# Scores in the groups' ring, late sum forms, a bias from a reversed table without transposes, and the mixers' fp32 products on fewer entries

## The chip, the cores and the metric

The kernel runs on one core of a Trainium2 chip. The metric is the device time of one execution in microseconds (us). The kernel before took 2042.75 us, the median of 3 runs (2042.73 to 2042.9). A profile is one more execution, taken by the hardware profiler, and it carries its own time.

## The reference

The block has one sequence of 256 frames with 2048 channels, all in fp32. A half-step SwiGLU FFN (2048 to 5632 and back) is followed by two token mixers side by side, a merge, a second half-step FFN and a last norm. The mixers are what the change touches:

```python
h = rmsnorm(x, norm_mix_g)
q_a, k_a, v_a, q_r, k_r, v_r, g_r, gate_a, gate_r = split(h @ w_in)
# attention: 8 heads of 128; chunks of 64 frames; a frame sees its whole chunk and the earlier chunks
scores = q_a k_a^T * 128 ** -0.5
rel_idx = clip(q_pos - k_pos, -128, 128) + 128
bias = rel_bias_table[:, rel_idx]              # table: 8 heads x 257
p = softmax(where(valid, scores + bias, -1e30))
att = p v_a
# retention: 8 heads of 128, rotary q and k, decay gamma_h ** |n - m|, the same chunk mask
ret = rmsnorm_per_head(sum over visible m of (q_r[n].k_r[m]) * decay * v_r[m])
merged = sigmoid(gate_a) * (att @ w_out_att) + sigmoid(gate_r) * ((silu(g_r) * ret) @ w_out_ret)
x = x + merged @ w_out
```

## The kernel before, in words

**Steps.** All large products run in fp32r: both factors are split in a high part (a rounded copy) and a low part (the rest), and three products (high by high, low by high, high by low: L148, L149, L151, in `three`) stand for one fp32 product. Weights come in slices of 256 rows by 512 columns (512 KB) on SyncE's queue (`fetch`); ScalarE makes the high part (L137), VectorE the low part (L138). One slice is one *step*: 12 matmuls of 512 columns on TensorE (a `Gemm` of 16 or 8 row blocks is 8 or 4 steps). A part of the GEMMs runs in *Strassen groups*, whose steps have 6 matmuls and need sums of weight slices and of activations instead. For these, copies of weight slices are loaded (L560, tiles named z...k and z...x) or added on the way (L565, L604) by GpSimd's DMA queue, and VectorE adds them (L549, L603, L617). There are 1080 steps.

**Order.** Every engine runs its instructions in the order in which the program writes them. The loop `run` goes over the steps: it first writes the splits for the step 4 ahead, then everything that is due at this step, in the order in which it was put on the list, and then the step's own products. `later(n, fn)` puts `fn` on the list for n steps later, and `at(step, fn)` for a given step. So all small work is placed by hand: its fp32 matmuls and transposes stand between the fp32r matmuls of two steps. Such a place is called an *entry* below.

**The mixers.** The steps that multiply with `w_in` begin at step 390. The last four projections, for retention (QR0, KR0, QR1, KR1, 8 steps each), begin at step 600, which is called M here. At M+32 begin the four output projections of attention (4 steps each), at M+48 those of retention, at M+64 the product with `w_out`, at M+96 the second FFN. In the stretch from M to M+48 the attention and the retention of all heads are inserted:
- Attention head h begins at M + HEAD_AT[h] (L48): `scores` (L966, L967: 256 and 128 columns of fp32 in a PSUM bank of the ring "side"; three VectorE operations scale the scores and add the bias), one step on `powers` (ScalarE), two on `shares` (VectorE), four on `transposes` (three, and a ScalarE copy at L1004), six on `values` (L1010, L1011).
- The results of a rotary projection are turned on VectorE and transposed by `to_transposed` (four transposes by L395 each) 3 and 4 steps after the projection's last step.
- Retention of four heads: b=0 is placed when KR0 is done and b=1 when KR1 is done, with a first wait RET_WAIT (L42). Head i has `scores` (L1035, L1036; VectorE multiplies by the decay at L1038 and L1039, giving the tile rp) at wait+2i, and `values` (L1048 to L1050, tile ro) three steps later. `finish`, at wait+9, for both halves of the frames: square (ScalarE), sum of squares (VectorE, L1060), a power on GpSimd (L386), and four VectorE products with the gate (L1066, tile rg). Three steps on, both halves of rg are transposed and split (`Operand.put`, tile retp).

**PSUM** has rings of banks: "acc" (3), "z" (3, used by the Strassen groups and by the second accumulator of ordinary jobs) and "side" (2, used by all the small work).

**The relative bias.** At 18 steps ahead of step 390, four DMAs of GpSimd's queue broadcast the 257 entries of two heads each to 128 partitions (`load_rel`); four steps later VectorE extends them to 384 entries (L344) and four DMAs (L349) write them to DRAM, as `rel_ext` [8, 128, 384]. Two DMAs at M-4 (L357, in `bias_transposed`) read that table with a row stride of 383, which gives the bias transposed (keys on partitions). From M on, `bias_natural` turns it: 16 transposes (L368, tile psb) at M to M+3, four at each step, four ScalarE copies (L374), four masking memsets (L375).

**Sums for Strassen.** A normalized activation operand (class `Norm`: n1, nm for the mixers, n2 for the second FFN) is written by `put` as transposed blocks b = 0 to 3. After each odd block, `add_up` makes four sum forms s5, s6, s3, s7 (L489 to L511), 1, 4, 7 and 10 steps later, each with one VectorE operation for the sum, a ScalarE copy for its high part 2 steps later, and a VectorE difference for its low part (L511) 3 steps later.

Of the kernel before, what the change touches and what calls it, by code (L numbers as in the profile page):

```python
# [8 lines left out]
F32 = mybir.dt.float32  # L9
F32R = mybir.dt.float32r  # L10
AF = mybir.ActivationFunctionType
ALU = mybir.AluOpType
# [3 lines left out]
P = 128  # L16
SEQ = 256
NT = SEQ // P
D = 2048
# [19 lines left out]
HALF_K = D // P // 2  # L39
LEAD = (10, 10)  # L40
MIX_LEAD = 6
RET_WAIT = (14, 5)  # L42
HELD = 6
MIX_ADDED = (0,)
FIRST_ADDED = (2, 3)
MIX_AHEAD = 12
FIRST_WAIT = 4
HEAD_AT = (3, 6, 10, 13, 17, 20, 24, 27)  # L48

MIX_SHARE = (0.5,) * 4 + (1.0,) * 4 + (0.0,) * 4 + (0.2,) * 4  # L50
# [33 lines left out]
def block_kernel(ctx: ExitStack, tc: tile.TileContext, x, g1, w1g, w1u, w1d, gm, w_in, rel, woa, wor, wo,  # L84
# [12 lines left out]
    def act_tile(dt, name):  # L97
        return apool.tile([P, 4, SEQ], dt, tag="act", name=name)
# [4 lines left out]
    def side_tile(name):  # L103
        return psum.tile([P, NB], F32, tag="side", name=name, bufs=2)
# [12 lines left out]
    def later(n, fn):  # L117
        due.setdefault(state["step"] + n, []).append(fn)
# [208 lines left out]
    nc.gpsimd.memset(mhalf, -0.5)  # L327

    rel_ext = dram.tile([HEADS, P, EXT], F32, name="rel_ext")
    REL_PAIR = 2  # L330

    def load_rel():

        tiles = []
        for h in range(0, HEADS, REL_PAIR):
            t = act_tile(F32, f"rel{h}").rearrange("p a q -> p (a q)")[:, : REL_PAIR * EXT]
            t = t.rearrange("p (h e) -> p h e", h=REL_PAIR)
            nc.gpsimd.dma_start(t[:, :, :NREL], rel[0, h : h + REL_PAIR, :].partition_broadcast(P))
            tiles.append(t)
        later(4, lambda: spread_rel(tiles))  # L340

    def spread_rel(tiles):
        for i, t in enumerate(tiles):
            nc.vector.tensor_copy(  # L344
                t[:, :, NREL:], t[:, :, NREL - 1 : NREL].to_broadcast([P, REL_PAIR, EXT - NREL])
            )

            dst = rel_ext[REL_PAIR * i : REL_PAIR * (i + 1)].rearrange("h p e -> p h e")
            nc.gpsimd.dma_start(dst, t)  # L349

    def bias_transposed():
        t = [act_tile(F32, f"biasT{half}") for half in range(2)]
        for half in range(2):
            src = bass.AP(
                rel_ext.tensor, rel_ext.offset + half * 4 * P * EXT + MAXREL, [[EXT - 1, P], [P * EXT, 4], [1, SEQ]]
            )
            nc.gpsimd.dma_start(t[half], src)  # L357
        return t

    def bias_natural(bt):  # L360
        for b in range(HEADS // 4):
            table["bias", b] = act_tile(F32, f"bias{b}")

        def turn(h):
            ps = side_tile(f"psb{h}")
            for i in range(2):
                for j in range(2):
                    nc.tensor.transpose(  # L368
                        ps[:, (2 * i + j) * P : (2 * i + j + 1) * P],
                        bt[(h + i) // 4][:, (h + i) % 4, j * P : (j + 1) * P],  # L370
                        id_sb,
                    )
            dst = table["bias", h // 4][:, h % 4 : h % 4 + 2, :]
            nc.scalar.copy(dst.rearrange("p h k -> p (h k)"), ps)  # L374
            nc.vector.memset(dst[0:CHUNK, :, CHUNK:P], MASKED)  # L375

        turn(0)
        for h in range(2, HEADS, 2):
            later(h // 2, lambda h=h: turn(h))


    def rsqrt(dst, ssum, n, width):

# [37 lines left out]
    class Norm:  # L421
# [40 lines left out]
        def put(self, b, halves=(0, 1)):  # L462
            if 0 in halves:
                self.raw[b] = act_tile(F32, f"{self.name}x{b}")
            raw = self.raw[b]
            for half in halves:
                ps = side_tile(f"{self.name}p{b}{half}")
                for i in range(2):
                    k = 4 * b + 2 * half + i
                    for t in range(NT):  # L470
                        nc.tensor.transpose(
                            ps[:, (2 * i + t) * P : (2 * i + t + 1) * P], xs[t][:, k * P : (k + 1) * P], id_sb
                        )
                for i in range(2):
                    k = 4 * b + 2 * half + i
                    nc.scalar.activation(
                        raw[:, 2 * half + i, :], ps[:, i * SEQ : (i + 1) * SEQ], AF.Copy, scale=self.gain[:, k : k + 1]
                    )
            k0, k1 = 2 * halves[0], 2 * halves[-1] + 2
            j = 4 * (b // 2)  # L480
            for t in range(NT):
                self.split_to(f"a{t}{b % 2}", slice(j + k0, j + k1), raw[:, k0:k1, t * P : (t + 1) * P])
            if 1 in halves and not self.sums:
                del self.raw[b]
            elif 1 in halves and b % 2 == 1:
                for i, key in enumerate(self.SUMS):
                    later(1 + 3 * i, lambda key=key: self.add_up(b // 2, key))

        def add_up(self, p, key):  # L489

# [420 lines left out]
    def ret_qk_done(key, b, after=None):  # L911
        def done(acc):
            srcs = []
            half = HD // 2

            def turn(t, s):
                r = tmp_tile(f"{key}{b}{t}r", "qk", 4)
                u = tmp_tile(f"{key}{b}{t}u", "scaled", 1)
                s4 = s.rearrange("p (h j d) -> p h j d", h=4, j=2)
                r4 = r.rearrange("p (h j d) -> p h j d", h=4, j=2)  # L920
                u4 = u.rearrange("p (h j d) -> p h j d", h=4, j=2)
                c = cos_sb[:, t, :].unsqueeze(1).to_broadcast([P, 4, half])
                n = sin_sb[:, t, :].unsqueeze(1).to_broadcast([P, 4, half])
                for j in range(2):
                    nc.vector.tensor_mul(r4[:, :, j, :], s4[:, :, j, :], c)
                    nc.vector.tensor_mul(u4[:, :, j, :], s4[:, :, 1 - j, :], n)
                nc.vector.tensor_sub(r4[:, :, 0, :], r4[:, :, 0, :], u4[:, :, 0, :])
                nc.vector.tensor_add(r4[:, :, 1, :], r4[:, :, 1, :], u4[:, :, 1, :])
                srcs.append(r)


            for t in range(NT):
                s = tmp_tile(f"{key}{b}{t}", "gate", 2)
                nc.scalar.activation(s, acc[t], AF.Copy, scale=nm.scale(t))
                later(1 + t, lambda t=t, s=s: turn(t, s))
            to_transposed(key, b, srcs, (3, 4))
            if after is not None:
                after()

        return done  # L940
# [17 lines left out]
    def attention(h):  # L958
# [3 lines left out]

        def scores():
            q, k = tposed["qa", b], tposed["ka", b]
            ps = side_tile(f"as{h}")
            nc.tensor.matmul(ps[:, 0:SEQ], q[:, i, P:SEQ], k[:, i, :], start=True, stop=True)  # L966
            nc.tensor.matmul(ps[:, SEQ : SEQ + P], q[:, i, 0:P], k[:, i, 0:P], start=True, stop=True)  # L967
            room = act_tile(F32, f"p{h}").rearrange("p a q -> p (a q)")
            s = room[:, : 3 * P].rearrange("p (j k) -> p j k", j=3)
            sm["room"] = room  # L970
            p3 = ps[:, : 3 * P].rearrange("p (j k) -> p j k", j=3)

            for j, bj in ((0, 1), (1, 0), (2, 0)):
                nc.vector.scalar_tensor_tensor(
                    s[:, j, :], p3[:, j, :], scale, table["bias", b][:, i, bj * P : (bj + 1) * P], op0=ALU.mult, op1=ALU.add
                )
            m = small.tile([P, NT], F32, tag="m", name="m")
            tot = small.tile([P, NT], F32, tag="l", name="l")
            for t, js in ((1, slice(0, 2)), (0, slice(2, 3))):
                nc.vector.reduce_max(m[:, t : t + 1], s[:, js, :], axis=AX.XY)  # L980
            nc.vector.tensor_scalar_mul(m, m, -1.0)
            sm["p"], sm["m"], sm["tot"] = s, m, tot
# [29 lines left out]
            hi, lo = att.alloc(b)  # L1012
            split_out(ps[:, :SEQ], hi[:, i, :], lo[:, i, :])

        return (0, scores), (1, powers), (2, shares), (4, transposes), (6, values)

    def all_attention():
        for h in range(HEADS):
# [3 lines left out]
    def retention(b):  # L1022
# [31 lines left out]
        def finish():  # L1054
            srcs = []
            for t in range(NT):
# [10 lines left out]
                        o[:, hs], outs[t][:, hs], rs[:, i : i + 1], nat["gr", b][:, t, hs], op0=ALU.mult, op1=ALU.mult  # L1067
                    )
                srcs.append(o)
            later(3, lambda: [ret.put(b, t, srcs[t]) for t in range(NT)])  # L1070

        for i in range(4):
            for s, stage in enumerate(head(i)):
                later(wait + 2 * i + 3 * s, stage)
        later(wait + 2 * 4 + 1, finish)

    w_in0 = w_in[0]

# [132 lines left out]
    def at(step, fn):  # L1211
        due.setdefault(step, []).append(fn)
# [45 lines left out]
    at(60, load_angles)  # L1258

    def set_bias():  # L1260
        bt = bias_transposed()
        later(4, lambda: bias_natural(bt))

    mix = next(c for c, s in enumerate(steps) if s.job.w is w_in0)
    at(mix - 18, load_rel)
    at(mix - 18, lambda: later(4, load_gain(gm, 1)))
    at(mixed - 4, set_bias)
    at(mixed - 3, lambda: bring_back(0))
    at(mixed + 5, lambda: bring_back(1))
    at(mixed, all_attention)  # L1270
    at(merges[0][0] + 4, lambda: later(8, load_gain(g2, 2)))
    at(mixed + 16, load_ret_gates)
    at(mixed + 20, set_decay)
    for step, fn in merges:
# [65 lines left out]
```

## Time and profile before

| | us |
|---|---|
| median of 3 runs | 2042.75 |
| the profiled execution's own time | 2042.8 |
| its span (first to last instruction) | 2041.0 |
| time around the span | 1.8 |
| TensorE busy in the span | 2028.7 |
| VectorE busy | 1786.4 |
| ScalarE busy | 1504.8 |
| GpSimd busy | 346.6 |

The page gives the busy time of every engine (PE is TensorE's matmuls, PEld its weight loads, DVE VectorE, ACT ScalarE, POOL GpSimd, SP SyncE), the span in 40 slices, and the chain of work that ended last. The trace behind it gives single instructions with their start, their duration and what ended the idle time ahead of them. TensorE's matmuls are pipelined, so that the duration of one overlaps the next: a matmul's price is read from start to start. The step M lies at about 1057 us, M+48 at about 1218 us.

### The profile page before, as it was taken

How to read it: one execution, taken by the hardware profiler on the slowest of the kernel's cores; microseconds unless marked ns; L12 is line 12 of the kernel's file. 1: busy time of each engine (PE TensorE's matmuls, PEld its weight loads, DVE VectorE, ACT ScalarE, POOL GpSimd, SP SyncE). 2: the span in 40 equal slices, each digit the busy share in tenths (PEclk: the TensorE clock that was granted, in tenths of full speed). 3: DMA queues.
4: the chain of work that ended last, by engine and by line, in shares of the span. 5: the costliest groups of instructions: out<-in, count | busy, mean ns of one | idle time of the engine just before them, and what ended most of it. 6: DMA issues, size and time to landing. Idle time of an engine off the chain costs nothing.

```text
span 2041.0 us, 26295 instructions
## 1 busy us (share of the span) xinstructions
PE 2028.7 (99%) x9188; PEld 1679.0 (82%) x9188; DVE 1786.4 (88%) x1835; ACT 1504.8 (74%) x1890; POOL 346.6 (17%) x405
## 2 busy tenths in 40 slices
PE   9999999999999999999999999999999999999998
PEld 7788888888888888888888888888888888888886
DVE  7999999999998899999987667569999999999996
ACT  7778887878887777777775434557788888888785
POOL 1221122212113021212120000011112221122200
PEclk9999999999999999999999999999999999999999
DMA  9888889988878689899896645576889988889974
GB/s 311 260 249 254 258 268 279 263 243 245 261 234 268 229 233 309 272 282 286 255 324 215 214 143 188 186 241 191 270 264 273 278 242 238 262 266 270 285 197 134
DMA packets 227141, 507.38 MB, mean 249 GB/s; under 512 B 15856, under 2 KB 16608, under 8 KB 227008
## 3 DMA queue, kind: packets, MB, share of 16 engines
q1 hardware_dynamic: 154560, 297.31, 43.1%
q0 software_dynamic: 68240, 199.41, 37.5%
q10 hardware_dynamic: 4208, 8.99, 1.2%
q8 instruction: 72, 1.18, 0.2%
q14 instruction: 61, 0.50, 0.1%
HBM read 472.08 MB, written 12.06 MB: 237 GB/s over the span
## 4 chain that ended last, share of the span: by engine, by line
PE 98%; DMA 1%; DVE 1%; ACT 0%; issue 0%; SPq 0%; DVEq 0%; POOLq 0%; POOL 0%; ACTq 0%
PE acc L151 15%; PE acc L148 15%; PE acc L149 15%; DMA raw<-in_ffn_w_gate_dram 1%; PE z390a L151 0%; PE z425a L149 0%; PE z814a L148 0%; PE z226a L148 0%; PE z958a L148 0%; PE z778a L148 0%; PE z82a L148 0%; PE z425a L148 0%; PE z154a L149 0%; PE z118a L149 0%; PE z298a L149 0%; PE z994a L149 0%
## 5 line engine op out<-in xcount | busy, mean ns | idle before, releaser
L138 DVE TENSOR_TENSOR lo<-raw,hi 128x1024 fp32r<-128x1024 f32 x351 | 427.1, 1219 | 121.4 <-ACT hi L137 118.5
L137 ACT CAST hi<-raw 128x1024 fp32r<-128x1024 f32 x351 | 367.8, 1050 | 184.7 <-PE acc L149 140.1
L828 ACT ACTIVATE xall<-acc 128x512 f32<-128x512 f32 x160 | 94.5, 591 | 13.1 <-PE acc L151 9.0
L825 ACT ACTIVATE acc<-xall 128x512 f32<-128x512 f32 x160 | 95.8, 599 | 2.5
L148 PE MATMUL acc<-hi,mgh 128*128 128x512 f32 x128 | 50.2, 392 | 0.0
L149 PE MATMUL acc<-hi,mgl 128*128 128x512 f32 x128 | 49.8, 389 | 0.0
L151 PE MATMUL acc<-lo,mgh 128*128 128x512 f32 x128 | 35.5, 389 | 0.0
L148 PE MATMUL acc<-hi,nma01h 128*128 128x512 f32 x80 | 32.5, 407 | 0.0
L148 PE MATMUL acc<-hi,nma00h 128*128 128x512 f32 x80 | 32.3, 404 | 0.0
L149 PE MATMUL acc<-hi,nma01l 128*128 128x512 f32 x80 | 31.3, 391 | 0.0
L149 PE MATMUL acc<-hi,nma11l 128*128 128x512 f32 x80 | 31.2, 390 | 0.0
L149 PE MATMUL acc<-hi,nma00l 128*128 128x512 f32 x80 | 31.2, 390 | 0.0
L148 PE MATMUL acc<-hi,nma11h 128*128 128x512 f32 x80 | 31.2, 390 | 0.0
L148 PE MATMUL acc<-hi,nma10h 128*128 128x512 f32 x80 | 31.2, 390 | 0.0
L149 PE MATMUL acc<-hi,nma10l 128*128 128x512 f32 x80 | 31.2, 390 | 0.0
L151 PEld LDWEIGHTS acc<-lo,mgh 128*128 128x128 f32 x128 | 24.0, 188 | 5.0
L148 PEld LDWEIGHTS acc<-hi,mgh 128*128 128x128 f32 x128 | 24.0, 188 | 4.9
L149 PEld LDWEIGHTS acc<-hi,mgl 128*128 128x128 f32 x128 | 24.0, 188 | 4.8
L148 PE MATMUL acc<-hi,atth 128*128 128x512 f32 x64 | 26.2, 410 | 0.0
L148 PE MATMUL acc<-hi,reth 128*128 128x512 f32 x64 | 25.3, 395 | 0.0
L149 PE MATMUL acc<-hi,attl 128*128 128x512 f32 x64 | 25.1, 392 | 0.0
L149 PE MATMUL acc<-hi,retl 128*128 128x512 f32 x64 | 24.9, 389 | 0.0
(6885 smaller groups left out, 7261.4 us busy)
## 6 DMA issues: line engine op xcount, KB each, us to landing
raw<-in_ffn_w_down_dram SPq DMA_DIRECT2D x176, 512.0 KB, 7.4
raw<-in_w_in_dram SPq DMA_DIRECT2D x80, 512.0 KB, 5.1
raw<-in_w_out_dram SPq DMA_DIRECT2D x32, 512.0 KB, 3.7
raw<-in_ffn_w_up_dram SPq DMA_DIRECT2D x16, 512.0 KB, 5.6
raw<-in_w_out_att_dram SPq DMA_DIRECT2D x16, 512.0 KB, 4.1
raw<-in_w_out_ret_dram SPq DMA_DIRECT2D x16, 512.0 KB, 3.9
raw<-in_ffn_w_gate_dram SPq DMA_DIRECT2D x15, 512.0 KB, 3.9
z390x<-in_w_in_dram POOLq DMA_DIRECT2D x8, 512.0 KB, 9.0
```

The costliest lines, as they stand in the source:

```text
L137: nc.scalar.copy(hi, raw)
L138: nc.vector.tensor_sub(lo, raw, hi.bitcast(F32))
L148: nc.tensor.matmul(acc, ahi, whi, start=first, stop=False, **more)
L149: nc.tensor.matmul(acc, alo, whi, start=False, stop=False, **more)
L151: nc.tensor.matmul(acc, ahi, wlo, start=False, stop=last, **more)
L825: nc.scalar.activation(acc, xs[t][:, cols], AF.Copy, scale=2.0)
L828: nc.scalar.activation(xs[t][:, cols], acc, AF.Copy, scale=0.5)
```

## The change

- The bias table is loaded once, to 8 partitions (one per head), in one DMA. Four steps later VectorE writes its reverse and an extension beside it, and one DMA writes `rel_ext`, each of the 8 rows 128 times. Two DMAs at M-6 now read the bias with queries on partitions. The transposes, the side banks and the copies are gone; two masking memsets, for four heads each, stand at M.
- Attention scores go to a bank of the ring "z" instead of "side". Two VectorE operations (256 and 128 columns) add the bias instead of three. `values` of heads 0 to 5 stands 7 steps after the scores instead of 6.
- The transposes of the rotary projections stand (6, 7), (5, 6), (4, 5) and (3, 4) steps after their projection, by ROTATED, instead of (3, 4) for all.
- RET_WAIT is (14, 6) instead of (14, 5). `values` of retention stands 2 steps after its scores instead of 3, `finish` at wait+8 instead of wait+9, and its two transposes 4 and 6 (b=0) or 3 and 3 (b=1) steps later instead of 3 and 3.
- The form s7 of the second pair of blocks is made 24 steps after `put` instead of 10, for nm and n2.
- A gain that is needed later (g2) is turned one step later.

```diff
-RET_WAIT = (14, 5)
+RET_WAIT = (14, 6)
+RET_PUT = ((4, 6), (3, 3))
+LAST_SUM = 24
+ROTATED = {("q", 0): (6, 7), ("k", 0): (5, 6), ("q", 1): (4, 5), ("k", 1): (3, 4)}
...
     def load_rel():
...
+        r = act_tile(F32, "rel").rearrange("p a q -> p (a q)")
+        raw, ext = r[:HEADS, :NREL], r[:HEADS, NB : NB + EXT]
+        nc.gpsimd.dma_start(raw, rel[0])
+        later(4, lambda: spread_rel(raw, ext))
+
+    def spread_rel(raw, ext):
+        nc.vector.tensor_copy(ext[:, P - 1 :], raw[:, ::-1])
+        nc.vector.tensor_copy(ext[:, : P - 1], raw[:, NREL - 1 :].to_broadcast([HEADS, P - 1]))
+        nc.gpsimd.dma_start(rel_ext, ext.unsqueeze(1).to_broadcast([HEADS, P, EXT]))
+
+    def load_bias():
         for b in range(HEADS // 4):
             table["bias", b] = act_tile(F32, f"bias{b}")
...
+            src = bass.AP(
+                rel_ext.tensor, rel_ext.offset + b * 4 * P * EXT + P - 1, [[EXT - 1, P], [P * EXT, 4], [1, SEQ]]
+            )
+            nc.gpsimd.dma_start(table["bias", b], src)
+
+    def mask_bias():
+        for b in range(HEADS // 4):
+            nc.vector.memset(table["bias", b][0:CHUNK, :, P + CHUNK :], MASKED)
...
-                    later(1 + 3 * i, lambda key=key: self.add_up(b // 2, key))
+                    wait = LAST_SUM if key == "s7" and self.name != "n1" and b == D // NB - 1 else 1 + 3 * i
+                    later(wait, lambda key=key: self.add_up(b // 2, key))
...
-            to_transposed(key, b, srcs, (3, 4))
+            to_transposed(key, b, srcs, ROTATED[key[0], b])
...
-            ps = side_tile(f"as{h}")
+            ps = acc_tile(f"as{h}", "z")
...
-            for j, bj in ((0, 1), (1, 0), (2, 0)):
+            bias = table["bias", b][:, i, :]
+            for cols, of in ((slice(0, SEQ), bias), (slice(SEQ, SEQ + P), bias[:, P:])):
                 nc.vector.scalar_tensor_tensor(
...
+                    room[:, cols], ps[:, cols], scale, of, op0=ALU.mult, op1=ALU.add
                 )
...
-        return (0, scores), (1, powers), (2, shares), (4, transposes), (6, values)
+        return (0, scores), (1, powers), (2, shares), (4, transposes), (6 + (h < HEADS - 2), values)
...
-            later(3, lambda: [ret.put(b, t, srcs[t]) for t in range(NT)])
+            for t in range(NT):
+                later(RET_PUT[b][t], lambda t=t: ret.put(b, t, srcs[t]))
 
         for i in range(4):
             for s, stage in enumerate(head(i)):
-                later(wait + 2 * i + 3 * s, stage)
-        later(wait + 2 * 4 + 1, finish)
+                later(wait + 2 * (i + s), stage)
+        later(wait + 2 * 4, finish)
...
     def set_bias():
-        bt = bias_transposed()
-        later(4, lambda: bias_natural(bt))
+        load_bias()
+        later(6, mask_bias)
...
-    at(mixed - 4, set_bias)
+    at(mixed - 6, set_bias)
...
-    at(merges[0][0] + 4, lambda: later(8, load_gain(g2, 2)))
+    at(merges[0][0] + 4, lambda: later(9, load_gain(g2, 2)))
```

More of the change, by code (lines that the diff above doesn't have):

```diff
@@ L329, in block_kernel @@
     rel_ext = dram.tile([HEADS, P, EXT], F32, name="rel_ext")
-    REL_PAIR = 2
     def load_rel():
[L334 to L360, printed above, removed]
+        r = act_tile(F32, "rel").rearrange("p a q -> p (a q)")
+        raw, ext = r[:HEADS, :NREL], r[:HEADS, NB : NB + EXT]
@@ L361, in bias_natural @@
+        nc.gpsimd.dma_start(raw, rel[0])
[5 more added lines that the diff above has]
+    def load_bias():
         for b in range(HEADS // 4):
             table["bias", b] = act_tile(F32, f"bias{b}")
[L364 to L375, printed above, removed]
@@ L377, in bias_natural @@
-        turn(0)
-        for h in range(2, HEADS, 2):
-            later(h // 2, lambda h=h: turn(h))
+            src = bass.AP(
[5 more added lines that the diff above has]
+            nc.vector.memset(table["bias", b][0:CHUNK, :, P + CHUNK :], MASKED)
     def rsqrt(dst, ssum, n, width):
@@ L970, in scores @@
             sm["room"] = room
-            p3 = ps[:, : 3 * P].rearrange("p (j k) -> p j k", j=3)
-            for j, bj in ((0, 1), (1, 0), (2, 0)):
+            bias = table["bias", b][:, i, :]
+            for cols, of in ((slice(0, SEQ), bias), (slice(SEQ, SEQ + P), bias[:, P:])):
                 nc.vector.scalar_tensor_tensor(
-                    s[:, j, :], p3[:, j, :], scale, table["bias", b][:, i, bj * P : (bj + 1) * P], op0=ALU.mult, op1=ALU.add
+                    room[:, cols], ps[:, cols], scale, of, op0=ALU.mult, op1=ALU.add
                 )
```

## The prediction, made before the changed kernel ran

> **What bounds the kernel now.** I read the view of cores first, then the page's busy times and its chain, then windows of the stretches that the change touches, and last single instructions of TensorE there.
>
> ```profile
> core 0: 2041.0 us, clock 0.999
> ```
> ```profile
> PE 2028.7 (99%) x9188; PEld 1679.0 (82%) x9188; DVE 1786.4 (88%) x1835; ACT 1504.8 (74%) x1890; POOL 346.6 (17%) x405
> ...
> PE 98%; DMA 1%; DVE 1%; ACT 0%; issue 0%; SPq 0%; DVEq 0%; POOLq 0%; POOL 0%; ACTq 0%
> ```
>
> TensorE is busy for 99% of the span, carries 98% of the chain, and its granted clock is 0.999: there is nothing to win from the clock, and work on another engine costs something only where TensorE comes to wait for it. A busy PE can still hide a wait, since the modelled ends of pipelined matmuls overlap it. So I price everything from start to start.
>
> ```profile
> 1055.30 0.62 PE L151 MATMUL z565a<-loz56533s,nma11h 128*128 128x512 f32 x2
> 1055.75 0.60 PE L368 MATMUL psb<-id_sb,biasT 128*128 128x128 f32 x4
> ...
> 1056.66 0.40 PE L148 MATMUL acc<-hi,nma00h 128*128 128x512 f32 x1
> ...
> 1057.58 0.40 PE L148 MATMUL acc<-hi,nma10h 128*128 128x512 f32 x1
> ...
> 1069.21 0.39 PE L148 MATMUL acc<-hi,nma00h 128*128 128x512 f32 x1
> ...
> 1071.93 0.39 PE L148 MATMUL acc<-hi,nma00h 128*128 128x512 f32 x1
> ...
> 1218.89 0.62 PE L151 MATMUL acc<-lo,atth 128*128 128x512 f32 x2
> 1219.35 1.04 PE L395 MATMUL retp<-id_sb,rg 128*128 128x128 f32 x8
> ...
> 1220.69 0.40 PE L148 MATMUL acc<-hi,reth 128*128 128x512 f32 x1
> ```
>
> From 1069.21 to 1071.93 stand the 12 matmuls of one undisturbed step: 2.72 us, 0.2267 each. From 1055.30 to 1056.66 (1.36 us) stand four of them and four bias transposes: four times 0.2267 is 0.907, so the transposes cost **0.453**. From 1218.89 to 1220.69 (1.80 us) eight transposes stand with four such matmuls, and cost 0.89. Two entries of four would cost 0.906, so one entry fewer saves about **0.01 us** when nothing waits in it. This is what gathering is worth by itself.
>
> VectorE matters in one stretch:
>
> ```profile
> 660.00:680.00 20.00, 20.00 (x98) 16.80 (x97) 11.58 (x13) 11.78 (x19) 1.92 (x3) 1.00 1.04 393
> 720.00:740.00 20.00, 20.00 (x91) 15.62 (x90) 20.00 (x21) 13.04 (x16) 2.44 (x2) 1.00 0.70 202
> ```
>
> The columns are the stretch, its length, the busy time of PE, PEld, DVE, ACT and POOL, the clock, the DMA share and GB/s. From 720 to 740 VectorE is busy for all 20.00 us and TensorE starts fewer matmuls (91 records, against 98).
>
> **The change part by part**, from the front of TensorE's queue.
>
> *A. The bias transposes.* Sixteen transposes in four places of four go: 4 x 0.453 = **-1.81**. The four copies and memsets went beside TensorE's work, so their going counts nothing; the new load stands two steps earlier, and its two DMAs have the same sizes and row stride.
>
> *B and D. Two waits that the profile shows.*
>
> ```profile
> 1088.34 0.30 PEld L966 LDWEIGHTS as<-ka0back,qa0back 128*128 128x128 f32 x2 [0.80 <-ACT p L1004]
> ...
> 1197.24 0.42 PEld L395 LDWEIGHTS retp<-id_sb,rg 128*128 128x128 f32 x4 [0.36 <-DVE rp L1039]
> ```
>
> Attention scores of head 2 wait 0.80 us for a bank of "side" that ScalarE has still to empty; in ring "z" there is another bank: **-0.80**. A transposed half of the retention waits 0.36 for a side bank that VectorE still reads; its entry is taken apart and stands later: **-0.35**. What is late next at both places is the following step's weights, which were not waited for at either.
>
> *C. Fewer entries.* By the list of steps I count 40 entries between M and M+48 before and 24 after. Three of the 16 that go belong to A (its fourth place is shared with scores); 13 x 0.01 = **-0.13**. The fp32 work that is left is the same in size.
>
> *E. The late sum.*
>
> ```profile
> 722.22 0.68 DVE L506 TENSOR_TENSOR nmf<-nmx 128x512 f32<-128x512 f32 x1
> 722.82 0.68 DVE L511 TENSOR_TENSOR nms3l<-nmf,nms3h 128x512 fp32r<-128x512 f32 x1
> ...
> 729.10 0.68 DVE L511 TENSOR_TENSOR nms7l<-nmf,nms7h 128x512 fp32r<-128x512 f32 x1
> ```
> ```profile
> 724.31 0.40 PE L148 MATMUL z390c<-hiz39010r,nms3h 128*128 128x512 f32 x1
> ...
> 747.96 0.39 PE L148 MATMUL z390b<-hiz39020r,nma01h 128*128 128x512 f32 x1
> ```
>
> Between these two starts (23.65 us) TensorE has 96 matmuls (21.76) and one group of eight transposes (0.89): 22.65, so it lost 1.00 us there, to splits of a full VectorE. Moving the sum s7 and its low part takes two operations out ahead of them, of 0.60 each from start to start (722.22 to 722.82). The gain is between 0 and 1.0; I take **-0.8**, nearest to the end at which the freed 1.2 us covers the whole loss. The low part then comes at 27 steps after `put`, five steps ahead of the first product that reads it (nine for n2), so it is not late. For n2 I find no loss to remove: 0.
>
> *F. A wait that is new.* With RET_WAIT at (14, 6) and `finish` at wait+8, three pieces fall due at the same step, M+37, in this order on the list: `values` of head 3, `finish` of b=0, `scores` of head 4. VectorE therefore does the whole finish (a sum, a wait for GpSimd's power, four products, and all of it again for the second half) ahead of the decay products of head 4; behind it in VectorE's queue are these and the following step's low part. `values` of head 4 on TensorE, which needs them, is now two steps later instead of three. The trace of before shows the same queue with head 5, which has three steps:
>
> ```profile
> 1184.94 0.38 PE L1048 MATMUL ro<-vr,rp 128*128 128x128 f32 x2
> ...
> 1189.02 0.38 PE L1048 MATMUL ro<-vr,rp 128*128 128x128 f32 x2
> ```
> ```profile
> 1192.59 0.41 DVE L1038 TENSOR_TENSOR rp<-rs,decay 128x256 f32<-128x256 f32 x1
> 1192.92 0.28 DVE L1039 TENSOR_TENSOR rp<-rs,decay 128x128 f32<-128x128 f32 x1
> ```
>
> The entry with `values` of head 3, `finish` and `scores` of head 5 begins at 1184.94. Its rp is done at 1192.92 + 0.28 = 1193.20, that is 8.26 after the entry's start. TensorE needs 4.08 us for such an entry and its step (1184.94 to 1189.02) and 2.72 for a second step: it stands at `values` of head 4 after 6.80. So it waits 8.26 - 6.80 = 1.46, with some tenths for the signal and for where the queue stands; I take **+1.7**, with 0 (the queue is shorter at that step) and 2.2 as ends. `finish` of b=1 has nothing behind it that is needed at once.
>
> *G. The rest.* By the list of steps the moved rotary transposes, the later `values` of attention and the gain's turn are 5 to 12 us of slack away from their next readers: 0, and at most some tenths if one of them isn't. The bias is read 6 steps (over 16 us) before its mask.
>
> Sum: -1.81 - 0.80 - 0.35 - 0.13 - 0.80 + 1.70 = **-2.2 us**. Against the profiled execution's own 2042.8 (its span 2041.0 and 1.8 around it) this gives 2040.6; that execution is 0.05 above the median of the runs, 2042.75, so I leave it at **2040.6**.
>
> **The rivals.**
>
> *1. The new wait is not there.* VectorE could do head 4's products in time if `finish` ran shorter at M+37. Then +1.7 falls out: 2042.8 - 3.9 = **2038.9**, and 2038.6 if E brings its whole 1.0 and 0.1 more comes from the entries. Against it stands the row of head 5, 8.26 us after its entry. Decides: rp earlier than 6.8 us after the start of the entry at M+37.
>
> *2. Slower: the table's write from eight partitions holds up the weights behind it.*
>
> ```profile
> 652.26 2.91 POOL L349 DMA_DIRECT2D rel_ext<-rel  x4 [20.89 <-DVE rel L344]
> ```
> ```profile
> 691.10 1.22 DVE L549 TENSOR_TENSOR z390x<-z390x,z390k 128x1024 f32<-128x1024 f32 x1
> ```
> ```profile
> rel_ext<-rel POOLq DMA_DIRECT2D x4, 384.0 KB, 7.8
> ```
>
> The same 1.57 MB (4 x 384 KB) now leave from 8 partitions instead of 128, in one transfer. Behind it in GpSimd's queue are the first weight copies of group z390, and VectorE first adds a pair of them at 691.10, shortly before it is full, when a delay passes on to TensorE. No row shows a transfer out of few partitions. The near end is as before, 7.8 us. The far end is 8/128 of the 393 GB/s that all transfers reached together from 660 to 680: 25 GB/s, 64 us. The write would end at 716 and the first pair land some 4 us later (1.05 MB at 393 GB/s is 2.7, and the issue), 29 us late; with 4 us of slack, since VectorE is busy for only 11.58 of the 20 us from 660 to 680, 2040.6 + 25 = **2065**. It decides from a write of about 35 us (652.26 + 35 + 4 = 691), or 45 GB/s; below 38 GB/s (41 us) the loss of 6 us makes the kernel slower by more than 0.2%. For it: eight rows are few. Against: it needs a rate nearer to the far end than to the near one.
>
> [...]
>
> *3. Ring "z" binds.* Scores in "z" could wait where a job's accumulators still hold its banks.
>
> ```profile
> 1059.99 0.69 ACT L1097 ACTIVATE sg<-z565a,nmrstd 128x512 f32<-128x512 f32 x1
> ```
>
> ScalarE still reads a z bank of the last group at 1059.99, while QR0 began its second accumulator, also in "z", at 1057.58 (row above): another bank was free, and a third one is there. If all the same two of the eight scores wait 0.8 us each, as the row of B did: 2040.6 + 1.6 = **2042.2**.
>
> **How the numbers follow.** A measurement of this kernel can tell about 0.2% from no change, 4.1 us: faster is below 2038.66, slower above 2046.84. The forecast as summed has 0.58, with 2039.3 to 2042 as its own range from the ends of E and F. Rival 1 has 0.22; its time lies at the bound, and with what the small terms may bring besides I put 0.14 of it below. Rival 2 has 0.14: 0.10 for a write slow enough to be slower by over 0.2%, 0.04 for a loss of 1 to 6 us. Rival 3 has 0.06. So faster 0.14, same 0.58 + 0.08 + 0.04 + 0.06 = 0.76, slower 0.10. The range from 2038.0 to 2044.0 leaves out some 0.05 below and, of rival 2, 0.12 above.
>
> **What would show it.** Right: no psb on TensorE around 1056; no wait at the second scores; the matmuls between the s3 product and the next group's first lose under 0.3 us instead of 1.00; the weight load of `values` of head 4 waits 1.3 to 2.2 us for VectorE's rp, near M+39; the table's write lands under 35 us. A wait for z390x at VectorE near 691 shows rival 2, scores that wait for ScalarE or VectorE in ring "z" rival 3. The prediction is wrong if any other wait of TensorE over 0.5 us appears between M and M+64, or if the stretches outside M to M+64 and 650 to 760 change by more than 0.5 us together.

## The result, and the profile after

The changed kernel takes **2063.6 us** (median of 4 runs, 2061.1 to 2065.76), the kernel before 2042.83 beside it. The ratio is 1.0099, with a 95% interval from 1.0087 to 1.0111: **slower by 1%**. The forecast of 2040.6 and its range to 2044.0 are missed; the prediction's rival 2 had named 2065, by another mechanism than the one that the traces show.

The profiled execution took 2061.1 us. Its view of cores, then the page's busy times and chain:

```profile
core 0: 2059.3 us, clock 0.994
```
```profile
PE 2031.7 (99%) x9172; PEld 1681.7 (82%) x9172; DVE 1785.9 (87%) x1823; ACT 1503.1 (73%) x1886; POOL 342.5 (17%) x399
...
PE 96%; DMA 2%; DVE 1%; ACT 0%; issue 0%; POOL 0%; SPq 0%; DVEq 0%; POOLq 0%; ACTq 0%
```

The 16 transposes fewer show in the counts (9172 against 9188). TensorE still reads 99% busy, although the span grew by 18.3 us, but only because the share is rounded: its idle time in the span grew from 12.3 us (2041.0 less 2028.7) to 27.6 (2059.3 less 2031.7), which is 15.3 of the 18.3. The chain points at the cause, with 96% on PE and 2% on DMA instead of 98% and 1%. The windows (columns as in the prediction) show where:

```profile
640.00:660.00 20.00, 20.00 (x90) 16.25 (x89) 13.85 (x16) 16.23 (x23) 6.10 (x8) 1.00 0.57 172
660.00:680.00 20.00, 16.80 (x73) 13.62 (x72) 4.87 (x5) 5.72 (x8) 0.00 (x0) 0.93 0.85 200
680.00:700.00 20.00, 10.42 (x40) 7.90 (x38) 6.07 (x7) 5.27 (x8) 0.00 (x0) 0.73 0.67 203
700.00:720.00 20.00, 19.06 (x89) 16.01 (x90) 16.50 (x23) 19.83 (x43) 2.38 (x2) 0.91 0.59 188
```

From 660 to 700 every engine runs out of work, and the DMA engines, 0.85 busy from 660 to 680, bring 200 GB/s where 393 came before. Next the issues of DMAs from 640 to 740 (KB each, and the median time from issue to landing):

```profile
raw<-in_ffn_w_down_dram SPq DMA_DIRECT2D x9, 512.0 KB, 22.6
...
z390k<-in_w_in_dram POOLq DMA_DIRECT2D x4, 512.0 KB, 40.5
...
rel_ext<-rel POOLq DMA_DIRECT2D x1, 1536.0 KB, 35.6
```

And the same from 640 to 700 in the kernel before (its four writes are in the prediction):

```profile
raw<-in_ffn_w_down_dram SPq DMA_DIRECT2D x9, 512.0 KB, 8.8
...
z390k<-in_w_in_dram POOLq DMA_DIRECT2D x4, 512.0 KB, 13.5
```

The table's write takes 35.6 us, from 652 to 688. Behind it in its queue the copies for group z390 take 40.5 us instead of 13.5. Beside it, on SyncE's queue, the ordinary slices of the down projection take 22.6 instead of 8.8. (These are medians of nine; the five slices issued after the write take 22.6 to 33.5 us, and those issued after the first of the writes of before 8.8 to 12.6.) ScalarE's splits and VectorE's first sum of copies show which of the two hurts, and TensorE's matmuls what it costs:

```profile
676.47 1.04 ACT L140 CAST hi<-raw 128x1024 fp32r<-128x1024 f32 x1 [9.56 <-DMA raw<-in_ffn_w_down_dram]
687.55 1.04 ACT L140 CAST hi<-raw 128x1024 fp32r<-128x1024 f32 x1 [10.03 <-DMA raw<-in_ffn_w_down_dram]
```
```profile
711.89 1.22 DVE L525 TENSOR_TENSOR z390x<-z390x,z390k 128x1024 f32<-128x1024 f32 x1
```
```profile
677.57 0.80 PE L151 MATMUL acc<-hi,f1a9h 128*128 128x512 f32 x1 [3.19 <-ACT hi L140]
...
690.50 2.35 PE L446 MATMUL nmp<-id_sb,xall 128*128 128x128 f32 x8 [8.50 <-DVE xall L666]
```

ScalarE waits some 10 us for each of two slices of `ffn_w_down`, and TensorE then waits for what is made of them. The copies for z390 are not waited for: VectorE first adds a pair of them at 711.89.

Both kernels have the same 8604 fp32r matmuls, so the n-th of one can be set against the n-th of the other. Each column is a place in the kernel before, in us; each row gives how much later the matmul that stands there starts in that kernel (the runs are described below).

| | 650 | 690 | 716 | 724 | 774 | 1056 | 1224 | 1440 | 1940 | end |
|---|---|---|---|---|---|---|---|---|---|---|
| after | -0.2 | +19.2 | +19.4 | +20.8 | +19.4 | +19.4 | +17.3 | +17.7 | +17.7 | +18.3 |
| e2_before_narrow | 0.0 | +20.0 | +21.6 | +23.0 | +22.9 | +22.9 | +22.9 | +22.9 | +22.9 | +23.1 |
| e3_eight_spread | -0.3 | -0.3 | -0.3 | +0.9 | -0.5 | -0.5 | -2.5 | -2.2 | -2.2 | -1.6 |
| e5_finish_later | 0.0 | 0.0 | 0.0 | +1.3 | -0.2 | -0.2 | -4.0 | -3.7 | -3.7 | -2.7 |
| e6_sums_early | -0.1 | -0.1 | 0.0 | +1.4 | +1.1 | +1.1 | -0.9 | -0.9 | -0.9 | -0.2 |
| e8_bias_alone | +0.5 | +0.5 | +0.9 | +2.2 | +1.8 | +1.8 | -0.1 | -0.1 | -0.1 | +0.8 |

The stretch of the write costs 19.4 us, more than the whole 18.3; the mixers (1056 to 1224) give 2.0 back.

### The profile page after: what moved, and what is told of

The parts are those of the page before. It is cut to its first block, busy times and chain, and to the rows that moved or that the text cites. A ratio compares the mean times of both kernels' runs of the same rounds, so it can differ in the third digit from the quotient of the medians.

```text
span 2059.3 us, 26221 instructions
## 1 busy us (share of the span) xinstructions
PE 2031.7 (99%) x9172; PEld 1681.7 (82%) x9172; DVE 1785.9 (87%) x1823; ACT 1503.1 (73%) x1886; POOL 342.5 (17%) x399
## 4 chain that ended last, share of the span: by engine, by line
PE 96%; DMA 2%; DVE 1%; ACT 0%; issue 0%; POOL 0%; SPq 0%; DVEq 0%; POOLq 0%; ACTq 0%
PE acc L154 15%; PE acc L151 15%; PE acc L152 15%; DMA raw<-in_ffn_w_down_dram 1%; DMA raw<-in_ffn_w_gate_dram 1%; PE z1030a L154 0%; PE z706a L151 0%; PE z425a L151 0%; PE z1030a L151 0%; PE z154a L151 0%; PE z886a L151 0%; PE z742a L151 0%; PE z298a L151 0%; PE z226a L152 0%; PE z190a L152 0%
## 5 line engine op out<-in xcount | busy, mean ns | idle before, releaser
L140 ACT CAST hi<-raw 128x1024 fp32r<-128x1024 f32 x351 | 367.7, 1050 | 201.5 <-PE acc L152 134.2
L804 ACT ACTIVATE xall<-acc 128x512 f32<-128x512 f32 x160 | 94.4, 590 | 13.4 <-PE acc L154 9.3
```

Of the source, the lines that this page charges most:

```text
L140: nc.scalar.copy(hi, raw)
L804: nc.scalar.activation(xs[t][:, cols], acc, AF.Copy, scale=0.5)
```

## The experiments

**Undoing the write's shape, and making it alone.** First theory (W): the write out of eight partitions slows the slices that travel beside it. Rival (G): the placing of the small work costs.

```diff
 # e1_wide_write, from the kernel after (excerpts)
-        nc.gpsimd.dma_start(rel_ext, ext.unsqueeze(1).to_broadcast([HEADS, P, EXT]))
+        nc.gpsimd.dma_start(rel_one, ext)
...
+            nc.gpsimd.dma_start(t, rel_one[h : h + 2, :].partition_broadcast(P))
...
+            nc.gpsimd.dma_start(rel_ext[2 * i : 2 * (i + 1)].rearrange("h p e -> p h e"), t)
...
-    at(mix - 18, load_rel)
+    at(mix - 22, load_rel)
 # e2_before_narrow, from the kernel before
...
+        nc.gpsimd.dma_start(r[:, :NREL], rel[0])
...
-            nc.gpsimd.dma_start(dst, t)
...
+        nc.gpsimd.dma_start(rel_ext, r.unsqueeze(1).to_broadcast([HEADS, P, EXT]))
```

> The changed kernel with one thing undone: the reversed table is written to DRAM once (12 KB), broadcast to 128 partitions and written from there in four transfers, as before the change, at the same step. Theory W (the write from eight partitions slows the weight slices that travel beside it): the loss of 19.4 us at the end of the first down projection is gone, and what is left is the rest of the prediction's sum as the trace of after shows it, 2041 to 2042 us. Theory G (the gathering and the late sums cost): the time stays at 2055 to 2064 us.

> The kernel before with one thing changed: the table, not reversed, is kept on eight partitions and written from there in one transfer; transposes and all else stay. Theory W: 2042.8 + 18 to 21 us, 2061 to 2064, with the loss between 670 and 690 us. Theory G: 2043 us, no change.

e2: 2065.27 us, ratio 1.011 (1.0096 to 1.0123), a little above W's range. Only the table's load, its extension and its write are changed in it. Its issues from 640 to 740:

```profile
raw<-in_ffn_w_down_dram SPq DMA_DIRECT2D x9, 512.0 KB, 28.0
...
rel_ext<-rel POOLq DMA_DIRECT2D x1, 1536.0 KB, 36.0
```

The write takes 36.0 us, and of the final +23.1 us +20.0 are there by 690, another 3.0 by 724. e1: 2045.97, ratio 1.0017 (1.0008 to 1.0026): the loss is gone but for some 4 us (W expected 2041 to 2042). Its four writes, issued from 656.85 to 660.98 (that of the change at 652.20), land in 6.8 us, but the four broadcast loads that this kernel needs (1.57 MB more, 8.7 us each) also travel beside the slices, which take 14.6 us; that these loads are what is left was not tried. W holds: the write alone brings the loss. G falls.

**What makes the write slow.** The same eight rows were put on other partitions, or four copies of each on 32, to tell the rows' places from their number and from the repeated reading of one row.

```diff
 # e3_eight_spread, from the kernel after (excerpts; e10_four_ports: two copies and ext[::2])
+            nc.gpsimd.dma_start(raw[4 * h : 4 * (h + 1)], rel[0, h, :].partition_broadcast(4))
...
-        nc.gpsimd.dma_start(rel_ext, ext.unsqueeze(1).to_broadcast([HEADS, P, EXT]))
+        nc.gpsimd.dma_start(rel_ext, ext[::4].unsqueeze(1).to_broadcast([HEADS, P, EXT]))
 # e4_32_rows (loaded as in e3)
...
+        dst = rel_ext.rearrange("h (c r) e -> (h c) r e", c=4)
+        nc.gpsimd.dma_start(dst, ext.unsqueeze(1).to_broadcast([4 * HEADS, P // 4, EXT]))
```

> The changed kernel, with the eight rows of the table on partitions 0, 4, 8 to 28 instead of 0 to 7, still eight rows and one transfer of the same packets. [...]

> The changed kernel, with the table four times on partitions 0 to 31, each of the 32 rows written 32 times in the one transfer. [...] If it is the repeated reading of the same row, in whatever number of rows, the write still takes over 25 us and the kernel over 2050.

> The changed kernel with the eight rows on partitions 0, 2, 4 to 14. [...]

The issues of e3, from 640 to 700:

```profile
raw<-in_ffn_w_down_dram SPq DMA_DIRECT2D x9, 512.0 KB, 9.5
...
rel_ext<-rel POOLq DMA_DIRECT2D x1, 1536.0 KB, 16.7
```

and those of e10:

```profile
raw<-in_ffn_w_down_dram SPq DMA_DIRECT2D x9, 512.0 KB, 12.9
...
rel_ext<-rel POOLq DMA_DIRECT2D x1, 1536.0 KB, 21.2
```

| rows on partitions | mean of a write's packet of 4608 bytes, us | write lands after, us | slices of `ffn_w_down`, us | kernel, us |
|---|---|---|---|---|
| 0 to 7 (after) | 0.62 | 35.6 | 22.6 | 2063.6 |
| 0, 2 to 14 (e10) | 0.28 | 21.2 | 12.9 | 2047.68 |
| 0, 4 to 28 (e3) | 0.18 | 16.7 | 9.5 | 2041.99 |
| 0 to 31, four copies (e4) | 0.24 | 13.4 | 13.8 | 2043.36 |
| 0 to 127, four writes (before) | 0.18 | 7.8 each | 8.8 | 2042.83 |

(The packets are those of the trace's DMA records; the slices are the median of the nine issued from 640 to 700. The kernels were timed in three groups, each beside the kernel before; the ratios allow for that.) Against the kernel before, e3 is 0.9996 (0.9987 to 1.0005), e4 1.0002 (0.9993 to 1.0011), e10 1.0025 (1.0015 to 1.0035). In e3 the eight rows, the packets and the single transfer of the write are those of the change; only the rows' places moved by up to 21 partitions (with a load in eight pieces), and a packet takes 0.18 us instead of 0.62. So neither the number of rows nor the repeated reading of a row makes the packets slow (if the reading did, e4 expected over 25 us for the write; it landed after 13.4), and e10 puts a point between. From the first packet to the last the write's 1.57 MB pass at 52 GB/s with the rows on partitions 0 to 7 (44 from issue to landing), at 101 with 0, 2 to 14 and at 133 with 0, 4 to 28. Why eight rows on neighbouring partitions give slow packets, no run shows. Landing earlier is not all that counts for the neighbours: e4 lands earlier than e3, but its slices take longer, 13.8 us, and the kernel is not faster.

**The same write at another time.**

```diff
 # e11_narrow_early, from the kernel after
-    at(mix - 18, load_rel)
+    at(mix - 31, load_rel)
```

> The changed kernel as it is, with rows on partitions 0 to 7, but the table loaded and written 13 steps earlier, near 600 us. Theory W: weight slices travel there too, so the write takes 35 us again and TensorE loses again, 8 to 20 us, somewhere between 605 and 650 us: 2050 to 2064. If the loss came from the loads of group z390 queued behind the write, as the prediction's rival 2 had it, these now have 35 us more, and the kernel takes about 2041.

2066.33 us, ratio 1.0116 (1.0102 to 1.0129). The write takes 34.8 us again, and the total is near W's, but the way is not. One wait of TensorE's weight loads between 630 and 662, and another from their list of waits from 560 to 760:

```profile
639.39 0.50 PEld L154 LDWEIGHTS z334a<-loz33421s,n1s7h 128*128 128x128 f32 x2 [3.39 <-DVE loz33421s L141]
```
```profile
PEld gps L308 <- issue: 19.4, 1, 19.4
```

and the issues from 636 to 645:

```profile
rel_ext<-rel POOLq DMA_DIRECT2D x1, 1536.0 KB, 34.8
...
grows<-in_norm_mix_g_dram POOLq DMA_DIRECT2D x1, 8.0 KB, 33.8
```

Here the 8 KB of the mixers' gain stand behind the write in GpSimd's queue, land after 33.8 us, and TensorE waits 19.4 for them (in the kernel after they stand ahead of the write). So this run does not tell W from the queue form of rival 2; it shows that the queue form exists, with another victim. It also shows a mishap: the table's load, 13 steps earlier in the program, is still issued only at 627.80 (627.24 in the kernel after), since it stands behind the loads of group z334 in GpSimd's queue. VectorE, whose reversal now comes earlier, waits 4.9 us for it, TensorE loses about 5 us ahead of the rest, and the write starts at 637.85, not near 600.

**The wait of step F.**

```diff
 # e5_finish_later, from e3_eight_spread
-RET_PUT = ((4, 6), (3, 3))
+RET_PUT = ((3, 5), (3, 3))
-        later(wait + 2 * 4, finish)
+        later(wait + 2 * 4 + (b == 0), finish)
```

> The changed kernel with the eight table rows on partitions 0, 4 to 28 (e3_eight_spread), and the finish of the first four retention heads one step later, behind the scores of head 4 (its two transposes stay where they were). Theory of step F of the prediction (head 4's decay products queue behind the finish on VectorE): the 1.87 us that TensorE loses ahead of the values of head 4 go, against e3_eight_spread -1.9, about 2040.1 us, and no other wait of over 0.5 us comes. Rival (another instruction is late next at the same place): -0.5 us or less.

2040.3 us, ratio 0.9986 (0.9977 to 0.9995): the lowest median of all. TensorE's weight loads in the kernel after show the wait, and VectorE what it waited for:

```profile
1206.12 0.30 PEld L1024 LDWEIGHTS ro<-vr,rp 128*128 128x128 f32 x2 [2.03 <-DVE rp L1014]
```
```profile
1204.61 1.13 DVE L1042 SCALAR_TENSOR_TENSOR rg<-ro,rs,gr 128x128 f32<-128x128 f32 x4 [1.12 <-POOL rs L361]
1205.65 0.41 DVE L1014 TENSOR_TENSOR rp<-rs,decay 128x256 f32<-128x256 f32 x1
1205.98 0.28 DVE L1015 TENSOR_TENSOR rp<-rs,decay 128x128 f32<-128x128 f32 x1
```

The decay products stand behind the finish's last product, as predicted. Start to start, without the fp32r matmuls beside it, the entry at 1206.12 costs 3.21 us; the same work without a wait costs 1.33 (the entry of 1184.94 before): a loss of 1.87. In e5 the offsets between 1180 and 1190 grow by 0.64 instead of 2.52 in e3, so 1.88 are gone, and no wait stands in its place.

**The late sum, the ring, the bias.**

```diff
 # e6_sums_early, from e3_eight_spread
+                    wait = 1 + 3 * i
 # e7_scores_side, from e3_eight_spread
+            ps = side_tile(f"as{h}")
 # e8_bias_alone: the kernel before, with load_rel (rows as in e3), load_bias and mask_bias of the change
```

> e3_eight_spread with the form s7 of the last blocks made 10 steps after the put again, for the mixers and the second FFN. Step E of the prediction (the late sum frees VectorE, worth 0.8 us at 716 to 748): 0.8 us slower than e3_eight_spread at the mixers, 0.4 faster at the second FFN. Rival (the late sum only moves the loss within the full stretch of VectorE): within 0.3 us at the mixers.

> e3_eight_spread with the attention scores back in the ring side, the gathered entries kept. If the z ring only spares the one wait of step B: +0.8 us. If the gathering needs it (values, transposes and scores, or values, scores and rotary transposes stand in one entry with two side banks, so the third waits for ScalarE or VectorE each time, 1 to 1.5 us in each of 8 entries): +8 to +12 us, about 2050 to 2054.

> The kernel before with the bias part of the change alone: reversed table, no transposes, loads two steps earlier, the table written from partitions 0, 4 to 28. Step A of the prediction: the four places of transposes go and nothing else moves, -1.81 us, about 2041.0. Rival (with the transposes gone, the next step's weights are what TensorE waits for): -0.5 us or less.

- e6: 2042.95 us, ratio 1.0 (0.9991 to 1.0009). From 724 to 774 TensorE gains 1.4 us in e3, with the late sum, and 0.3 in e6, without it: the late sum is worth 1.1 at the mixers. At the second FFN (1425 to 1440) it costs 0.35. Step E was right in kind; it is no mere shift.
- e7: 2047.59 us, ratio 1.0023 (1.0014 to 1.0032), 5.6 more than e3. The waits of TensorE's weight loads from 1050 to 1260:

```profile
PEld as L943 <- ACT p L981: 3.2, 3, 1.6
...
PEld qr1p L371 <- DVE attl L366: 0.8, 1, 0.8
PEld kr0p L371 <- DVE attl L366: 0.8, 1, 0.8
PEld qr0p L371 <- DVE attl L366: 0.8, 1, 0.8
```

  Six entries wait, not eight, and for less than expected, but the gathering needs the third ring.
- e8: 2043.25 us, ratio 1.0001 (0.9992 to 1.001), where 2041.0 was expected; in this kernel two blocks of the bias stand in each other's place, with the same operations and sizes. Between 1056 and 1068 it gains 1.90 us, as step A had it (1.81). But it stands 0.5 behind already at 650, loses 1.3 more by 774, near 720 (below), and 0.9 near 1950.

**A best version.** e5 with the form s7 late for nm alone and the table written earlier: e9_best changes both at once, and e12_best_mended makes the reversal later.

```diff
 # e9_best, from e5_finish_later
-    at(mix - 18, load_rel)
+    at(mix - 31, load_rel)
-... self.name != "n1" and ...
+... self.name == "nm" and ...
 # e12_best_mended, from e9_best
-        later(4, lambda: spread_rel(raw, ext))
+        later(14, lambda: spread_rel(raw, ext))
```

> The version to which the runs point: table rows on partitions 0, 4 to 28, the table loaded and written 13 steps earlier (near 600 us, where the DMA engines carry 188 GB/s instead of 393), the finish of the first heads one step later, the late form s7 for the mixers alone. If the 1.1 to 1.4 us that every version with the one-transfer write loses near 720 come from the slices which that write delays, they go, and with e5_finish_later's account (about -4.2 between 1055 and 1220 and -1.4 from the late sum) the kernel takes 2036.5 to 2038. If they do not come from it, 2039 to 2040.5.

> e9_best with one mend: VectorE reverses the table 14 steps after the load instead of 4, so that it no longer waits 8.99 us for a load that GpSimd's queue holds back behind the accumulating loads of group z334. The write then starts near 641 us, where the DMA engines are busy for 0.21 of the time (640 to 650 in e3_eight_spread). Without that wait (+8.97 at 635 to 640) the account of e9_best is -4.5 against before: 2038.0 to 2038.8 us. If the write disturbs the slices at its new place, over 2040.

e9: 2047.25 us, ratio 1.0021 (1.0012 to 1.003), a miss. VectorE waited for the table's load, which GpSimd's queue held back:

```profile
DVE rel L342 <- DMA rel<-in_rel_bias_dram: 9.0, 1, 9.0
```

That cost 8.96 between 635 and 640. But from 716 to 724, where the kernel after, e1 to e8, e10 and e12 lose 1.1 to 1.4 us, e9 loses nothing (-0.06); its write was over at 655. e12: 2041.18, ratio 0.9991 (0.9982 to 1.0000), a miss as well: its write started at 649, not 641, landed after 14.6 us, and the slices took 12.1; TensorE lost 1.6 us at 670 to 680 and 1.1 near 720. So e5 has the lowest time, 2.5 us under the kernel before; e12 is 1.9 under the kernel before beside it, and their intervals overlap.

## Why the prediction was wrong

- **The step that failed** is the price of the table's write: the sum has no term for it, so it was taken at nothing, and the write was argued only as rival 2, with a chance of 0.14. The runs show 19.4 us in its place, in two parts that failed differently. The first is the rate. The rival asked whether the write takes over 35 us, and gave this little chance because it "needs a rate nearer to the far end than to the near one"; measured are 35.6 us, 44 GB/s. The second is the victim. The bound was drawn for the z390 copies behind the write in GpSimd's queue. These came 27 us late, and nothing waited for them, though here the 19 us that TensorE had lost by then helped. Without that they would have cost little: the first pair landed at 691.86, against the sum at 691.10 in the kernel before, and the next two pairs (695.91 and 699.96) ahead of the sums that need them there (697.82 and 703.70). What bound were the slices of SyncE's queue, which travelled in the meantime: 22.6 us instead of 8.8. For these a write under the bound of 35 us is not harmless either, as e10 shows: 21.2 us cost 5.1 by 690. That the rival's 2065 is near the measured 2063.6 is luck: it came from a write of 64 us and another victim.
- **Steps A, B, D and F** held. A: -1.90 for -1.81 (e8). B and D: the waits of 0.80 and 0.36 are gone from the profile. F: +1.87 for +1.70, at the place and for the reason named (e5).
- **Step C** was mis-sized, as far as a difference can tell. The mixers changed by -2.02 (1056 to 1224), where A to D and F sum to -1.39. With F at +1.87 the gains are 3.89; A's 1.90 and the two waits' 1.15 leave 0.84 for 13 entries, 0.06 each instead of 0.01. If all of it belongs to the entries, the price from one joined pair was too low; no run took the gathering alone, so this stays open.
- **Step E** was right at the mixers (1.1 for 0.8) and wrong at the second FFN (+0.35 for 0).
- **Not foreseen:** the 1.1 to 1.4 us near 720. They stand also in e2 and e8, which have none of the new sums, and in e1, whose write leaves from 128 partitions, and not in e9 and e11. In e3 ScalarE splits a slice at 679.22 that it splits at 678.31 in the kernel before, 0.9 us later, and VectorE, full from 700, carries that on. That the write's traffic delays that slice is argued, not shown: e12, whose write was over at 664, loses them too, and in e9 and e11 TensorE had lost some 9 us and more shortly before, in which slices could catch up. From 1940 to 1960 all kernels of the table but e2 lose 0.6 to 1.0; the cause was not tried. With the 0.35 of the second FFN this is more than the 0.5 us that the prediction allowed outside its stretches. Each of these figures is from one execution.

## What to carry to other kernels

Price a transfer by the partitions that it leaves from, not by its size alone (here 1.57 MB landed after 35.6 us from partitions 0 to 7 and after 16.7 from 0, 4 to 28), and charge it to all that travels in the meantime (here slices of another queue, 22.6 us instead of 8.8), not only to what stands behind it in its queue. If a few rows must be written many times, put them on partitions that lie apart: here four copies of each row and `[::4]` were worth some 21 us. Before a piece of work is moved ahead of another on the same engine, ask who needs what now stands behind it; that part of the prediction came out to 0.2 us.

## What the runs showed of the hardware

- The write out of eight neighbouring partitions held DMA engines rather than leaving them free: in the window from 660 to 680 they are 0.85 busy at 200 GB/s, in the kernel before 1.04 at 393. The write's 336 packets of 0.62 us in 30 us (656.8 to 687.1) are 7 at a time; in e3 they are 5 at a time (in 11.6 us), with 0.18 us each. The slices' own packets of 2048 bytes take no longer beside it, 0.09 us both in the kernel after and beside the four writes of before; but while the write runs they bring 77 GB/s instead of 140. That the slices wait for their turn at the engines would fit this; no run shows it.
- The eight-row writes (after, e2, e3, e10) never have more than 9 packets in flight at a time; the four writes of before and the 32 rows of e4 have up to 18 and 17. An estimate from 9 against 18 is that such a write has about half of the DMA engines that the four writes have. The 9 holds for e3 too, so it is not what made the write of the change slow. Whether it is why e3 passes 133 GB/s and the four writes of before 250 was not tried.
- Behind the long waits of these traces TensorE was slow for some us. Its matmuls behind the last of three long waits in the kernel after:

```profile
700.94 1.88 PE L446 MATMUL nmp<-id_sb,xall 128*128 128x128 f32 x8 [1.90 <-ACT nmx L451]
702.47 0.78 PE L151 MATMUL acc<-hi,f1a9h 128*128 128x512 f32 x1
703.05 0.63 PE L152 MATMUL acc<-hi,f1a9l 128*128 128x512 f32 x1
703.48 0.63 PE L151 MATMUL acc<-hi,f1a9h 128*128 128x512 f32 x1
703.90 0.63 PE L152 MATMUL acc<-hi,f1a9l 128*128 128x512 f32 x1
704.33 0.70 PE L154 MATMUL acc<-lo,f1a9h 128*128 128x512 f32 x2
704.87 0.40 PE L151 MATMUL acc<-hi,f1a9h 128*128 128x512 f32 x1
705.11 0.40 PE L152 MATMUL acc<-hi,f1a9l 128*128 128x512 f32 x1
```

  The six matmuls from 702.47 to 704.87 take 2.40 us instead of 1.36; the granted clock is 0.56 from 702.4 to 704.8 and 1.00 from 705 to 710. (Around the ends of the other two waits, at 677.57 and 690.50, it is 0.50 from 677.2 to 680.6 and from 684.1 to 694.2.) Behind each of the nine waits of 1.90 to 19.0 us in the traces (the kernel after, e2, e9, e10, e11), the first six such matmuls take 2.27 to 2.73 us; behind each of the twelve waits of 0.90 to 1.61 us after the first 20 us, 1.46 to 1.49. So each of the nine cost 0.9 to 1.4 us more than its wait shows. The wait of 1.90 ends 10 us after one of 8.50; the shortest of the slow ones that no other wait precedes is 2.97.
